# A streaming encoder layer on one core: norm statistics and small level products issued in portions, mixer weights split in the first FFN, scores three blocks ahead

## The chip, the cores and the metric

The kernel runs on one core of a Trainium2 chip. The metric is the device time of one execution in microseconds; several executions are timed, and their median counts. One more execution is profiled: every instruction of the engines TensorE (PE, with its weight loads as PEld), VectorE (DVE), ScalarE (ACT), GpSimd (POOL) and the DMA queue of SyncE (SP) is recorded.

## What is computed

One inference step of an encoder layer on 1056 tokens (1024 of a prompt and 32 of a running stream), width 1024, all in fp32:

```python
x = x + 0.5 * swiglu(rmsnorm(x, g_ffn1), w1g, w1u, w1d)
mix, k, v, s = token_mixer(rmsnorm(x, g_mix), w_in, ...)
x = x + mix
x = x + 0.5 * swiglu(rmsnorm(x, g_ffn2), w2g, w2u, w2d)
return rmsnorm(x, g_final), k, v, s
...
def token_mixer(h, ...):
    q_sb, k_sb, v_sb, q_g, k_g, v_g, r_g, lr_g = jnp.split(h @ w_in, points, axis=-1)
    o_sb = rmsnorm(stick_breaking(rmsnorm(q_sb), rmsnorm(k_sb), v_sb))   # 8 heads x 64
    o_g = rmsnorm(gla_scan(q_g, k_g, v_g, log_a)) * silu(r_g)            # 4 heads, dk 64, dv 128
    return concat(o_sb, o_g) @ w_out
```

Stick-breaking attention takes, for each query, a sigmoid of each score times the product of (1 - sigmoid) over all later keys. The gated linear attention (GLA) is a scan over tokens with a decay for each key channel.

## The kernel before

**Number format.** Activations lie transposed: eight tiles `S.x[d]` of 128 channels x 1056 tokens. Matmuls take fp32r operands, and each fp32 operand is split into a high and a low half by `split_to`: ACT rounds to the high half, then DVE (or POOL, with `pool=True`) subtracts to get the low one. A product is three matmuls (`mm3`, L60 to L62): high x high, high x low, low x high.

**Stages.** First FFN (gate and up by Strassen steps in `gate_up`, then down), the mixer, the second FFN. In the mixer a slab of `w_in` (128 output channels, one of 24) is used by one projection (`proj`, tile `pj`): three chunks of 352 tokens, each eight `mm3`. `load_split` brings a slab as 512 KB into `S.raw`, and splits it into `whl`, one of two buffers of the pool `wp`; in the mixer the low half is POOL's (L53).

**What sets the order.** `run(items, filler)` issues a list of items (small dependent pieces: scores, transposes, level products) and strews fillers (one `mm3` of a projection, or one output group) among them in proportion to the weights given. Behind it the framework's scheduler may still reorder instructions that are ready. Each engine then runs its own queue strictly in that order, and SP issues all DMAs of the kernel in its own.

**GLA.** `gla_items` treats two heads at a time: the decay logits, then products of queries and keys at levels 6 to 0 (`level6` and `level5` as one piece each, on operands `M`), then states and outputs. It runs twice, with projections as filler.

**Attention.** Four pairs of heads, p = 0 to 3. `sb_project` makes q, k and v of the next pair as filler, while `sb_items` runs sixteen blocks of the current one. A `Block` has three parts: `scores` (matmuls `z`, two sigmoids on ACT, a scan L1206 and a product L1207 on DVE that give `w`), `turn` (transposes `tr` of `w`, split into `wt`) and `values` (matmuls `av`). Scores are issued two blocks ahead of the turns; `f` and `w` have two buffers each.

**Norms.** `Norm.stat` squares a head's output, sums over channels by nine narrow matmuls (`means`, tile `st`, L711, 18 in the profile), takes the power -1/2 on POOL (L701) and for pairs of heads spreads the result (L729). `Norm.apply` transposes it (L746) and multiplies (L749). Both are one piece each.

**The end of the mixer.** When the third pair is done, the gated GLA heads in `S.x[4..7]` are split into `S.h[4..7]`, all twelve pieces at once. During the fourth pair output groups (`out_group`, tile `po`, on slabs `wo` loaded and split by `slab_a`) are the filler, and `ready(k)` splits finished heads, one POOL operation each (L53, tile `h`).

**First FFN.** In `gate_up` each step has seven products (24 matmuls each, tiles `acc_a` to `acc_d`); the hidden parts that the down product needs are formed (`keep`), split and stored to `part_spill`, four of them in one burst after a step's last product, through four buffers `S.x[0..3]`.

Of the kernel before, what the change touches and what calls it, by code (L numbers as in the profile page):

```python
# [15 lines left out]
P = 128  # L16
# [21 lines left out]
def load_split(S, src, hi_pool, tag, pool=False):  # L38
# [5 lines left out]
    split_to(S, w[:, 0], w[:, 1], raw, pool)  # L44
    return w

# [227 lines left out]
class Step:  # L274
# [89 lines left out]
    def out(self, q, u, ps):  # L364
# [12 lines left out]
        else:  # L377
# [9 lines left out]
            if f in PLAIN:  # L387
                nc.sync.dma_start(S.hidden[PLAIN.index(f)][:, h * HALF : h * HALF + HALF], hid)
            elif q != 1:
                self.keep({0: "B11", 3: "B22", 2: "B21"}[q], hid)  # L390
            else:
                b11, b12, b21, b22 = (S.x[4 + n][:, :HALF] for n in range(4))
                for name, o, x, y in (("T1", b11, b12, b11), ("T3", b12, b22, b12), ("T2", b22, b22, b11), ("T4", b21, b21, b22)):
                    nc.vector.tensor_sub(o, x, y)  # L394
                    self.keep(name, o)

    def keep(self, name, src):
# [16 lines left out]
def gate_up(S, H, op, steps, among, between, tail, xd):  # L414
# [31 lines left out]
    for t in range(N):  # L446
        for p in ORDER:
            steps[t].product(p)
            steps[t].after(p)
            if p > 2:  # L450
# [217 lines left out]
def proj(S, src, cb):  # L668
# [4 lines left out]
    def one(c, k):  # L673
        def go():
            if "w" not in hold:
                hold["w"] = load_split(S, src, S.wp, "w", True)
# [28 lines left out]
def means(S, sq, ones, groups):  # L705

    nc = S.nc
    st = S.pst.tile([P, CW], F32, name="st", tag="st")
    for b in range(NB + 1):
        n = P if b < NB else DEC  # L710
        nc.tensor.matmul(st[:n, groups * b : groups * b + groups], sq[:, b * P : b * P + n], ones[:, :: P // groups], start=True, stop=True)  # L711
    return rsqrt(S, st, groups)


class Norm:
# [6 lines left out]
    def stat(self):  # L722
        S = self.S
        sq = square_buf(S)
        S.nc.scalar.activation(sq, self.t, AF.Square)
        self.r = means(S, sq, self.ones, self.groups)
        if self.groups > 1:
            r, f = self.r, P // self.groups
            spread = lambda t, r: S.nc.gpsimd.tensor_copy(t.rearrange("p b (g f) -> p b g f", f=f), r.unsqueeze(3).broadcast_to([*r.shape, f]))  # L729
            big = S.nbuf[1] if S.nbuf else S.big.tile([P, NR], F32, name="nR", tag="b")  # L730
            self.r = big[:, :SEQ].rearrange("p (b f) -> p b f", f=P)
            self.last = S.tmp.tile([DEC, 1, P], F32, name="nL", tag="nL", bufs=1)
            spread(self.r, r[:, :NB])
            spread(self.last, r[:DEC, NB:])
# [15 lines left out]

    def parts(self):
        return [(4, self.stat), (4, self.apply)]
# [55 lines left out]
def gla_qk(S, A, hp):  # L808
    nc = S.nc
    qg, kg = S.x[4 + 2 * hp], S.x[5 + 2 * hp]  # L810
    q = proj(S, A["win"][12 + hp], lambda c, ps: nc.scalar.activation(qg[:, cs(c)], ps, AF.Copy, scale=0.125))
    k = proj(S, A["win"][14 + hp], lambda c, ps: nc.vector.tensor_copy(kg[:, cs(c)], ps))
# [3 lines left out]
def gla_v(S, A, hp, vs):  # L816
# [11 lines left out]
    return [proj(S, A["win"][16 + 2 * hp + h], put(h)) for h in range(2)]  # L828


def gla_items(S, A, G, hp, vs):
# [54 lines left out]
    def level6():  # L886
        M, ps = T.M[6], pair("g6")
        for b in range(NB):
            o = b * P
            for h in range(2):  # L890
# [870 lines left out]
```

## Time and profile before

| | us |
|---|---|
| three runs: median (lowest to highest) | 2154.25 (2153.37 to 2156.0) |
| profiled execution, its own time | 2149.15 |
| its span, first to last instruction | 2147.4 |
| mean granted clock of TensorE | 0.988 |

The profile's page gives each engine's busy time, and groups of instructions by line; "idle before" is the engine's idle time just ahead of a group and what ended it. The windows view gives busy time in stretches of the span, and the clock that was granted there. The timeline lists instructions in order, with the idle time before each in brackets. Lines (L53) are those of the kernel before.

### The profile page before, as it was taken

What the parts mean: (1) busy time and instruction counts of PE and PEld (TensorE: products, weight loads), DVE (VectorE), ACT (ScalarE), POOL (GpSimd) and SP (SyncE); (2) the same over time, 40 slices, a digit from 0 to 9 for tenths busy, and PEclk for the clock granted to TensorE, in tenths of its full rate; (3) what the DMA queues carried; (4) which work ended last, traced back from release to release, by engine and by line L of the source; (5) the groups of instructions that cost most, each with busy time, mean ns of one, the idle gap of its engine ahead of it and who ended that gap; (6) DMA issues with size and microseconds to landing.
All of it is one profiled execution on the core that took longest, in us unless ns stands there. A gap on an engine that the chain in (4) does not pass through costs nothing.

```text
span 2147.4 us, 38446 instructions
## 1 busy us (share of the span) xinstructions
PE 2069.2 (96%) x15636; PEld 1998.0 (93%) x15636; DVE 1442.3 (67%) x2142; ACT 892.2 (42%) x1586; POOL 742.8 (35%) x609
## 2 busy tenths in 40 slices
PE   7999999999999999999999988899999999999997
PEld 6899999999999978888888987899999999999997
DVE  6856756646786766286776687687567667467865
ACT  6533433432233443335555555454334333322333
POOL 0134334345872321122223312101343343458720
PEclk9999999999999999999999999999999999999999
DMA  5134434449823200102203141231344334498322
GB/s 174 50 120 152 161 121 154 168 139 379 303 94 117 87 32 30 38 31 67 77 23 100 36 124 69 78 123 51 120 159 156 127 143 168 139 376 300 106 65 82
DMA packets 106705, 270.49 MB, mean 126 GB/s; under 512 B 10432, under 2 KB 31200, under 8 KB 106528
## 3 DMA queue, kind: packets, MB, share of 16 engines
q1 hardware_dynamic: 106528, 268.03, 35.6%
q8 instruction: 123, 2.02, 0.4%
q14 instruction: 54, 0.44, 0.1%
HBM read 174.46 MB, written 86.77 MB: 122 GB/s over the span
## 4 chain that ended last, share of the span: by engine, by line
PE 77%; DVE 13%; ACT 3%; issue 3%; DMA 2%; POOL 1%; DVEq 0%; SPq 0%; ACTq 0%; POOLq 0%
PE acc_a L335 11%; PE acc_c L335 11%; PE acc_d L335 11%; PE acc_b L335 5%; PE acc L243 4%; PE pj L60 3%; PE pj L61 3%; PE pj L62 3%; PE pd_c L516 3%; PE pd_a L516 2%; PE pd_d L516 2%; DVE f L1206 2%; PE pd L60 2%; PE pd L62 2%; PE pd L61 2%
## 5 line engine op out<-in xcount | busy, mean ns | idle before, releaser
L335 PE MATMUL acc_a<-h,whl 128*128 128x264 f32 x1920 | 250.1, 286 | 1.8 <-DVE whl L55 1.8
L335 PE MATMUL acc_d<-part,S 128*128 128x264 f32 x1920 | 246.6, 284 | 0.0
L335 PEld LDWEIGHTS acc_a<-h,whl 128*128 128x128 f32 x1920 | 241.6, 190 | 2.1 <-DVE whl L55 2.1
L335 PEld LDWEIGHTS acc_d<-part,S 128*128 128x128 f32 x1920 | 238.7, 188 | 0.0
L60 PE MATMUL pj<-h,whl 128*128 128x352 f32 x576 | 203.9, 354 | 0.0
L61 PE MATMUL pj<-h,whl 128*128 128x352 f32 x576 | 191.1, 332 | 0.0
L62 PE MATMUL pj<-h,whl 128*128 128x352 f32 x576 | 190.8, 331 | 0.0
L51 ACT ACTIVATE S<-s 128x512 fp32r<-128x512 f32 x160 | 98.7, 627 | 183.6 <-PE acc_d L335 77.0
L51 ACT ACTIVATE x<-x 128x528 fp32r<-128x528 f32 x112 | 72.4, 647 | 180.8 <-DVE x L394 84.8
L319 POOL TENSOR_TENSOR s<-wraw,s 128x512 f32<-128x512 f32 x38 | 49.1, 1292 | 278.9 <-DVE S L55 278.9
L385 POOL TENSOR_TENSOR x<-tc,x 128x528 f32<-128x528 f32 x60 | 103.6, 1727 | 120.0 <-DVE tc L384 107.4
L53 POOL TENSOR_TENSOR whl<-wraw,whl 128x1024 fp32r<-128x1024 f32 x28 | 69.4, 2480 | 169.9 <-ACT whl L51 169.8
L55 DVE TENSOR_TENSOR x<-x 128x528 fp32r<-128x528 f32 x112 | 85.3, 761 | 63.1 <-ACT x L51 60.8
L335 PE MATMUL acc_b<-h,S 128*128 128x264 f32 x960 | 125.5, 286 | 1.5 <-ACT h L51 1.1
L335 PE MATMUL acc_c<-part,S 128*128 128x264 f32 x960 | 124.3, 284 | 0.3 <-DVE hid L255 0.3
L55 DVE TENSOR_TENSOR S<-s,S 128x512 fp32r<-128x512 f32 x160 | 122.0, 763 | 3.7 <-ACT S L51 2.5
L335 PE MATMUL acc_c<-h,A 128*128 128x264 f32 x960 | 124.2, 285 | 0.0
L335 PEld LDWEIGHTS acc_b<-h,S 128*128 128x128 f32 x960 | 121.2, 189 | 1.9 <-ACT h L51 1.3
L534 POOL TENSOR_TENSOR x<-x,u 128x528 f32<-128x528 f32 x64 | 103.5, 1624 | 49.5 <-DVE x L505 49.0
L335 PEld LDWEIGHTS acc_c<-part,S 128*128 128x128 f32 x960 | 120.0, 188 | 0.6 <-DVE hid L255 0.6
L335 PEld LDWEIGHTS acc_c<-h,A 128*128 128x128 f32 x960 | 120.4, 188 | 0.0
L306 POOL TENSOR_TENSOR s<-wraw 128x512 f32<-128x512 f32 x38 | 48.9, 1288 | 195.6 <-DVE S L55 195.6
(344 smaller groups left out, 5122.4 us busy)
## 6 DMA issues: line engine op xcount, KB each, us to landing
part_spill<-x SPq DMA_DIRECT2D x112, 528.0 KB, 2.8
h<-part_spill SPq DMA_DIRECT2D x64, 528.0 KB, 8.9
part<-part_spill SPq DMA_DIRECT2D x48, 528.0 KB, 9.6
wraw<-win SPq DMA_DIRECT2D x24, 512.0 KB, 3.4
wraw<-w1g SPq DMA_DIRECT2D x22, 512.0 KB, 3.7
wraw<-w1u SPq DMA_DIRECT2D x22, 512.0 KB, 3.4
wraw<-w1d SPq DMA_DIRECT2D x22, 512.0 KB, 3.8
wraw<-w2g SPq DMA_DIRECT2D x22, 512.0 KB, 3.5
```

Of the source, the lines that this page charges most:

```text
L51: nc.scalar.activation(hi, src, AF.Copy)
L53: nc.gpsimd.tensor_sub(lo, src, hi.bitcast(F32))
L55: nc.vector.tensor_sub(lo, src, hi.bitcast(F32))
L60: nc.tensor.matmul(out, w[:, 0, wsl], a[:, 0, asl], start=first, stop=False)
L61: nc.tensor.matmul(out, w[:, 0, wsl], a[:, 1, asl], start=False, stop=False)
L62: nc.tensor.matmul(out, w[:, 1, wsl], a[:, 0, asl], start=False, stop=last)
L243: nc.tensor.matmul(out, self.w[i](k, a), quarter(S, k, b, j), start=k == 0 and n == 0, stop=k == KT - 1 and n == 2)
L319: eng.tensor_sub(src, a12, self.s2)
L335: nc.tensor.matmul(t[:, s, :SW], w[:, a, ks], m(k, b, s), start=fresh and k == 0 and n == 0, stop=k == 3 and n == 2, skip_group_check=not ...
L385: nc.gpsimd.tensor_mul(two(hid), t, sg)
L516: nc.tensor.matmul(t[:, s, :SW], w[:, u, k * P : k * P + P], b[:, v, ss(s)], start=fresh and k == 0 and i == 0, stop=k == 1 and i == 2, sk ...
L534: nc.gpsimd.tensor_add(x[r][h], x[r][h], u)
```

## The change

It has six parts.

1. `Splits` takes 26 slabs in the first FFN's loop (22 of `w_in`, all but those of the first GLA q and k, and the first four of `w_out`), as 52 halves: load of 256 KB, split on ACT and DVE, store of 512 KB to `win_split` or `wo_split`, at slots counted in products. Its two buffers are `S.x[2]` and `S.x[3]`.
2. In the mixer `load_halves` loads a split slab, 1 MB, straight into `whl`. `S.raw` is only open in the FFNs, and its room goes to a third buffer of `f` and `w`.
3. `form` spreads the hidden parts over the following two steps, through two buffers.
4. `means` and `Norm.stat` return three items of three matmuls each, and `spread_in` puts them among the projections. `level6` and `level5` become items of four blocks, and a pad of weight 24 stands before them in the first GLA run.
5. Scores run three blocks ahead.
6. The gated heads are split by chunk in the filler (`gated`), the finished heads by chunk on DVE (`ready(k, c)`), and the third pair's norm is spread among the output groups.

```diff
+def load_halves(S, src, pool, tag):
+    w = pool.tile([P, 2, 1024], F32R, name="whl", tag=tag)
+    S.nc.sync.dma_start(w.bitcast(F32), src)
+    return w
...
+class Splits:
+        for n in range(2 * len(jobs)):
+            slot = 5 * n // 2
+            for k, fn in ((0, self.load), (3, self.split), (4, self.store)):
+                self.at.setdefault(slot + k, []).append((fn, n))
...
+    def load(self, n):
+        self.S.nc.sync.dma_start(self.buf(n)[:, 512:], self.jobs[n // 2][0][:, self.cols(n)])
+    def split(self, n):
+        t = self.halves(n).bitcast(F32R)
+        split_to(self.S, t[:, 0], t[:, 1], self.buf(n)[:, 512:])
+    def store(self, n):
+        self.S.nc.sync.dma_start(self.jobs[n // 2][1][:, :, self.cols(n)], self.halves(n))
...
-        t = S.x[S.n_kept % 4].bitcast(F32R).rearrange("p (a n) -> p a n", a=2)
+        t = S.x[S.n_kept % 2].bitcast(F32R).rearrange("p (a n) -> p a n", a=2)
...
+FORMS = [{1: [(1, "B21")], 3: [(1, "T1")], 5: [(1, "T3")]}, {0: [(2, "T2")], 2: [(2, "T4")], 4: [(0, "B22")], 6: [(0, "B11")]}]
...
+            for back, name in FORMS[t % 2].get(n, ()):
+                if t >= back:
+                    steps[t - back].form(name)
...
+            chore(7 * t + n)
...
+    def some(b0):
+        def go():
+            for b in range(b0, b0 + 3):
+                nc.tensor.matmul(out, hold["sq"][:, b * P : b * P + n], ones[:, :: P // groups], start=True, stop=True)
+            if b0 == 6:
+                put(rsqrt(S, hold["st"], groups))
+        return 2, go
+    return [some(b0) for b0 in (0, 3, 6)]
...
+def spread_in(items, at, step, more):
+    for n, x in enumerate(more):
+        items.insert(at + n * (step + 1), x)
...
-    items += [(6, level6), (6, level5)]
+    if not early:
+        items.append((24, lambda: None))
+    items += [(3, level6(b0)) for b0 in (0, 4)] + [(3, level5(b0)) for b0 in (0, 4, 8, 12)]
...
+    spread_in(pk[0], 2, 3, means(S, lambda: T.sq, S.ones64, 2, scales))
+    for n in norms[1:]:
+        spread_in(pk[1], 0, 3, n.stat())
+        pk[2][4:4] = [(4, n.apply)]
...
-        if n + 2 < len(blocks):
-            items.append((w, blocks[n + 2].scores))
+        if n + 3 < len(blocks):
+            items.append((w, blocks[n + 3].scores))
...
+            jobs = [(A["win"][i], A["win2"][i]) for i in range(24) if i not in (12, 14)]
+            jobs += [(A["wo"][i], A["wo2"][i]) for i in range(4)]
+            splits = Splits(S, jobs, (S.x[2], S.x[3]))
...
+                def gated(c):
+                    for k in (6, 7, 4, 5):
+                        split_to(S, hi, lo, o)
...
-                S.att, S.big, S.wt = pool("att", 2), pool("big", 2), pool("wt", 3)
-                fills = [gate(2), gate(0), gate(1) + gate(3)]
+                S.att, S.big, S.wt = pool("att", 2), pool("big", 3), pool("wt", 3)
+                g1, g3 = gate(1), gate(3)
+                fills = [flat(gate(2)), flat(gate(0)), flat([g1[c] + g3[c] + [(0, lambda c=c: gated(c))] for c in range(NCH)])]
...
-                        slabs[j] = load_split(S, A["wo"][j], S.wp, "w", True)
+                        slabs[j] = load_halves(S, A["wo2"][j], S.wp, "w")
...
-                            split_to(S, S.h[k][:, 0], S.h[k][:, 1], S.x[k], True)
+                        def ready(k, c):
+                            split_to(S, S.h[k][:, 0, cs(c)], S.h[k][:, 1, cs(c)], S.x[k][:, cs(c)])
...
+                        spread_in(fill, 1, 1, prev.stat() + [(4, turned)])
+                        for n in range(9):
+                            fill.insert(10 + n, (1, lambda n=n: ready(n // 3, n % 3)))
```

Where the scheduler puts this, three places show. POOL's queue in the second half of the attention, before (`whl` is a slab's low half, `f` a block's border, `nr` and `nv` the power of a norm):

```order
L1194 MEMSET f 128x1 x5
L53 TENSOR_TENSOR whl<-wraw,whl 128x1024
L1194 MEMSET f 128x1
L53 TENSOR_TENSOR whl<-wraw,whl 128x1024
L1194 MEMSET f 128x1
L701 TENSOR_TENSOR nr<-nv,mhalf 128x18
L729 COPY x<-nr 128x1024
L729 COPY nL<-nr 32x128
L697 MEMSET nv 128x18
L1194 MEMSET f 128x1 x4
L1249 MEMSET fs 32x2
L53 TENSOR_TENSOR whl<-wraw,whl 128x1024
```

And POOL after the change, at the same place:

```order
L1302 MEMSET f 128x1 x5
L759 TENSOR_TENSOR nr<-nv,mhalf 128x18
L812 COPY x<-nr 128x1024
L812 COPY nL<-nr 32x128
L755 MEMSET nv 128x9
L1302 MEMSET f 128x1 x4
L1357 MEMSET fs 32x2
L1302 MEMSET f 128x1 x2
L759 TENSOR_TENSOR nr<-nv,mhalf 128x18
L1201 TENSOR_SCALAR rn<-nr 128x18
L755 MEMSET nv 128x18
```

The slab splits are gone; what is left on POOL is borders, powers and copies. Next TensorE in the attention of the second pair, before (`st` is a statistic, `tr` and `av` the turns and values, `z` scores, `pj` a projection):

```order
L1218 MATMUL tr<-consts,w 128x128
L711 MATMUL st<-consts,x 128x2 x8
L711 MATMUL st<-consts,x 32x2
L1231 MATMUL av<-wt,vs 128x256 x14
L1231 MATMUL av<-wt,vs 128x128 x2
L1199 MATMUL z<-ks,qh 128x384
L1200 MATMUL z<-ks,ql 128x384
L1202 LDWEIGHTS identb
L1202 MATMUL z<-maskb,identb 128x128
```

TensorE after the change, around the second portion of the same kind of statistic:

```order
L103 MATMUL pj<-h_86,whl 128x352
L104 MATMUL pj<-h_86,whl 128x352
L105 MATMUL pj<-h_86,whl 128x352
L1307 MATMUL z<-ks,qh 128x512
L1308 MATMUL z<-ks,ql 128x512
L1310 LDWEIGHTS identb
L1310 MATMUL z<-maskb,identb 128x128
L1326 MATMUL tr<-consts,w 128x128 x2
L777 MATMUL st<-consts,x 128x2 x3
L103 MATMUL pj<-h_87,whl 128x352
L104 MATMUL pj<-h_87,whl 128x352
L105 MATMUL pj<-h_87,whl 128x352
```

The nine matmuls of the statistic stood in one run, and now come as three, three and three, some twenty instructions apart. In the GLA runs they still stand in one run of nine. Last DVE at the end of the third pair, before (`h_88` to `h_91` are `S.h[4..7]`, split in chunks of 352; `ks` is the next pair's key; L1517 and L1518 are a gate):

```order
L1137 TENSOR_TENSOR ks<-kf,ks 64x1056
L55 TENSOR_TENSOR wt<-tr,wt 128x4x128
L55 TENSOR_TENSOR h_90<-x,h_90 128x352
L55 TENSOR_TENSOR h_88<-h_88 128x352
L55 TENSOR_TENSOR h_89<-h_89 128x352
L55 TENSOR_TENSOR h_88<-h_88 128x352
L55 TENSOR_TENSOR h_89<-h_89 128x352
L1178 TENSOR_TENSOR x<-avt,av 64x256
L1517 TENSOR_TENSOR rs<-rs,pj 128x352
L55 TENSOR_TENSOR h_88<-h_88 128x352
L1518 TENSOR_TENSOR x<-x,rs 128x352
L55 TENSOR_TENSOR h_89<-h_89 128x352
```

DVE after the change, where the first chunk's gated heads are split:

```order
L1628 TENSOR_TENSOR rs<-rs,pj 128x352
L98 TENSOR_TENSOR h_90<-x,h_90 128x352
L1629 TENSOR_TENSOR x<-x,rs 128x352
L98 TENSOR_TENSOR h_88<-h_88 128x352
L98 TENSOR_TENSOR h_89<-h_89 128x352
L98 TENSOR_TENSOR h_91<-x,h_91 128x352
L1286 TENSOR_TENSOR x<-avt,av 64x256
L1244 TENSOR_TENSOR ks<-kf,ks 64x1056
L98 TENSOR_TENSOR h_85<-x,h_85 128x352
L1314 SCALAR_TENSOR_TENSOR f<-f 128x1024
L98 TENSOR_TENSOR wt<-tr,wt 128x4x128
L1315 TENSOR_TENSOR w<-w,f 128x1024
```

The splits of the gated heads stood next to each other behind the last `wt` splits; now each chunk's four come with its gate, among scans and `wt` splits, and pieces of `h_84` and `h_85` (the finished heads, POOL's before) lie between them.

More of the change, by code (lines that the diff above doesn't have):

```diff
@@ L411, in gate_up_steps, with gate_up @@
     return steps
-def gate_up(S, H, op, steps, among, between, tail, xd):
+def gate_up(S, H, op, steps, among, between, tail, xd, chore):
     N = len(steps)
@@ L702, in rsqrt, with means @@
     return r
-def means(S, sq, ones, groups):
+def means(S, sq, ones, groups, put):
     nc = S.nc
[L708 to L712, printed above, removed]
+    hold = {}
+    def some(b0):
+        def go():
+            if b0 == 0:
+                hold["sq"] = sq()
+                hold["st"] = S.pst.tile([P, CW], F32, name="st", tag="st")
+            for b in range(b0, b0 + 3):
+                n = P if b < NB else DEC
+                out = hold["st"][:n, groups * b : groups * b + groups]
+                nc.tensor.matmul(out, hold["sq"][:, b * P : b * P + n], ones[:, :: P // groups], start=True, stop=True)
[6 more added lines that the diff above has]
+        items.insert(at + n * (step + 1), x)
 class Norm:
@@ L826, in put @@
         return cb
[L828 removed]
+    return [proj(S, A["win2"][16 + 2 * hp + h], put(h)) for h in range(2)]
 def gla_items(S, A, G, hp, vs):
@@ L884, in pair @@
         return [S.pz.tile([P, 512], F32, name=name, tag="z") for _ in range(2)]
[L886 to L890, printed above, removed]
-                nc.tensor.matmul(ps[h][:64, b * 64 : b * 64 + 64], M[HS[h], o : o + 64], M[HS[h], o + 64 : o + P], start=True, stop=True)
-        for h in range(2):
-            nc.scalar.activation(T.AT[h][0:64, 0:NB, 64:P], ps[h][:64].rearrange("p (b t) -> p b t", b=NB), AF.Copy)
-        ahead(4)
@@ new lines, in level5, with go @@
+    def level5(b0):
+        def go():
+            if b0 == 0:
+                T.ps = pair("g5")
+            M, ps = T.M[5], T.ps
+            for b in range(b0, b0 + 4):
+                o = b * 64
+                for h in range(2):
+                    nc.tensor.matmul(ps[h][:32, b * 32 : b * 32 + 32], M[HS[h], o : o + 32], M[HS[h], o + 32 : o + 64], start=True, stop=True)
+            if b0 == 12:
+                for h in range(2):
+                    p4 = ps[h][:32].rearrange("p (b two t) -> p b two t", two=2, t=32)
+                    nc.scalar.activation(T.AT[h][0:32, 0:NB, 32:64], p4[:, :, 0], AF.Copy)
+                    nc.scalar.activation(T.AT[h][64:96, 0:NB, 96:P], p4[:, :, 1], AF.Copy)
+                ahead(3)
+        return go
@@ L1450, in between @@
                     emit(parts(H))
-            gate_up(S, H, op, steps, among, between, down.head, A["x"])
+            jobs = [(A["win"][i], A["win2"][i]) for i in range(24) if i not in (12, 14)]
+            jobs += [(A["wo"][i], A["wo2"][i]) for i in range(4)]
+            splits = Splits(S, jobs, (S.x[2], S.x[3]))
+            gate_up(S, H, op, steps, among, between, down.head, A["x"], splits.some)
             nc.vector.tensor_copy(S.identb, consts[:, 0])
@@ L1648, in between @@
                     emit(parts(H))
-            gate_up(S, H, op, steps, lambda j, n: [], between, down.head, xs)
+            gate_up(S, H, op, steps, lambda j, n: [], between, down.head, xs, lambda n: None)
             down.strassen(xs)
```

179 lines of the change are left out of this document (103 added, 76 removed).

## The prediction

> **What bounds the kernel now.** I read the page first, for the engine that sets the time.
>
> ```profile
> PE 2069.2 (96%) x15636; PEld 1998.0 (93%) x15636; DVE 1442.3 (67%) x2142; ACT 892.2 (42%) x1586; POOL 742.8 (35%) x609
> ```
>
> TensorE is busy for 96% of the span, and the change takes no matmul away (in the order of instructions the mixer has 1836 wide and 1710 small ones before and after). So it can win only TensorE's idle time and time at a lowered clock. The windows view, cut at the first scores of each pair of heads, tells where those are; its columns are stretch, length, busy us of PE, PEld, DVE, ACT and POOL, granted clock, DMA share and GB/s.
>
> ```profile
> 100.00:480.00 380.00, 380.00 (x3118) 380.00 (x3118) 236.03 (x302) 144.66 (x226) 157.08 (x107) 1.00 0.40 143
> 745.00:893.00 148.00, 139.89 (x957) 122.61 (x956) 79.49 (x126) 55.31 (x85) 28.55 (x16) 0.99 0.09 29
> 893.00:988.00 95.00, 91.74 (x672) 78.65 (x671) 65.93 (x124) 39.44 (x60) 19.40 (x15) 0.96 0.15 50
> 988.00:1076.00 88.00, 82.91 (x571) 76.02 (x571) 66.30 (x100) 53.71 (x113) 23.56 (x30) 1.00 0.23 65
> 1076.00:1167.00 91.00, 88.14 (x591) 81.02 (x591) 66.30 (x101) 53.37 (x112) 26.97 (x34) 0.96 0.15 47
> 1167.00:1284.00 117.00, 110.03 (x730) 103.68 (x729) 86.24 (x126) 66.02 (x136) 33.23 (x35) 0.97 0.31 88
> 1284.00:1378.00 94.00, 84.71 (x546) 76.17 (x544) 67.13 (x107) 47.32 (x99) 20.12 (x24) 0.95 0.15 53
> ```
>
> The first FFN's loop (first row) has no TensorE idle at all: nothing to win there, only to lose. The six mixer stages idle for 8.1, 3.3, 5.1, 2.9, 7.0 and 9.3 us, 35.6 in all, and their clock is below 1. That is the purse. Cut finer, the lowered clock turns out to be eight short windows at half rate between 745 and 1378:
>
> ```profile
> 1081.40:1084.80 3.40, 3.40 (x14) 3.40 (x13) 1.94 (x4) 1.19 (x3) 3.34 (x2) 0.50 0.27 104
> 1136.00:1139.40 3.40, 3.40 (x13) 2.81 (x12) 2.59 (x4) 2.54 (x5) 3.34 (x2) 0.50 0.00 0
> 1224.70:1228.10 3.40, 3.40 (x15) 3.34 (x14) 0.99 (x3) 0.60 (x1) 2.73 (x4) 0.51 0.00 0
> 1279.40:1286.20 6.80, 6.67 (x26) 6.60 (x27) 4.50 (x11) 3.48 (x8) 0.00 (x0) 0.50 0.67 239
> 1293.00:1296.40 3.40, 3.35 (x13) 2.90 (x14) 1.72 (x4) 0.00 (x0) 2.61 (x4) 0.50 0.14 20
> 1320.30:1323.70 3.40, 3.37 (x14) 2.91 (x13) 3.40 (x5) 1.64 (x3) 0.00 (x0) 0.50 0.01 5
> 791.30:794.70 3.40, 3.29 (x36) 2.72 (x35) 3.40 (x3) 1.72 (x3) 2.45 (x1) 0.51 0.00 0
> 900.50:907.30 6.80, 6.80 (x29) 6.25 (x30) 4.15 (x6) 1.75 (x2) 1.91 (x2) 0.50 0.15 59
> ```
>
> Half rate costs half the window: 1.7 us for 3.4, 3.4 for 6.8, 17 us in all. Idle and clock together are 52.6 us: no outcome of this change can win more than about that.
>
> **The change part by part.** *Splits off POOL (pre-split weights).* In the mixer POOL makes the low half of each slab, and DVE wants the same stretch of time. First at 993, in the timeline (start, length, engine, idle before and who ended it):
>
> ```profile
> 992.26 2.38 POOL L53 TENSOR_TENSOR whl<-wraw,whl 128x1024 fp32r<-128x1024 f32 x1
> 993.06 1.86 DVE L1206 TENSOR_TENSOR_SCAN f<-f 128x128 f32<-128x128 f32 x1 [1.57 <-ACT f L1203]
> 995.49 0.30 PE L1218 MATMUL tr<-consts,w 128*128 128x128 f32 x1 [1.46 <-DVE w L1207]
> ```
>
> ```profile
> 1288.47 0.40 DVE L1206 TENSOR_TENSOR_SCAN f<-f 128x128 f32<-128x128 f32 x1
> ```
>
> The same scan takes 0.40 us elsewhere and 1.86 beside a split: it ends with the POOL operation, and TensorE waits the 1.46 us that it grew by. Two more such places, the first in the linear attention, the second in the last pair:
>
> ```profile
> 792.17 2.86 DVE L876 TENSOR_TENSOR M<-M,x 128x512 f32<-128x512 f32 x1
> 795.17 1.51 PE L901 MATMUL g<-M 64*32 64x32 f32 x64 [0.58 <-DVE M L876]
> 798.88 1.30 PE L925 MATMUL gr<-M 64*128 64x128 f32 x11 [1.04 <-DVE M L876]
> ```
>
> ```profile
> 1315.79 2.79 DVE L1207 TENSOR_TENSOR w<-w,f 128x896 f32<-128x896 f32 x1
> 1319.37 0.44 PE L1218 MATMUL tr<-consts,w 128*128 128x128 f32 x2 [2.37 <-DVE wt L55]
> 1354.06 1.08 DVE L1207 TENSOR_TENSOR w<-w,f 128x896 f32<-128x896 f32 x1
> ```
>
> L1207 grew by 2.79 - 1.08 = 1.7 us. All slab splits but those of the first q and k leave the mixer, so these waits go: 1.46 + 0.58 + 1.04 + 1.7 = **4.8 us**. What is late next at 1319 is the scan itself, and the 0.7 left of that wait I leave standing.
>
> The price is paid in the first FFN: 52 half slabs, each a split on ACT and DVE and two DMAs.
>
> ```profile
> L55 DVE TENSOR_TENSOR S<-s,S 128x512 fp32r<-128x512 f32 x160 | 122.0, 763 | 3.7 <-ACT S L51 2.5
> part_spill<-x SPq DMA_DIRECT2D x112, 528.0 KB, 2.8
> ```
>
> A split of that shape takes DVE 0.763 us: 52 make 40 us, or 80 if each were held up to twice its length beside POOL, and DVE's 236 of 380 us become 276 (316). ACT, at 145, gets no more than that. Both keep gaps. The halves move 52 x 0.79 MB = 41 MB, 107 GB/s on top of 143, so a DMA share near 0.70 by the row's 0.40. A half comes every 2.5 products of 24 matmuls (380 / 3118 x 24 = 2.9 us by the first row of the windows), and an accumulator is next written two products after its last read is due; that 5.9 us is the cover. If it failed, every wait there would add to the end. I take 0 (the row's idle time is 0), with 10 us as the high end. The hidden parts, split in one burst before, are spread over two steps and use two buffers instead of four; a store lands in 2.8 us and a buffer comes round after four products, so that is 0 too.
>
> In the mixer a slab's load is now 1 MB and starts only when the slab two before it is done. Counted in the order, with 0.16 us for a wide matmul (the 0.122 of the first windows row x 352/264), this leaves 14 us or more, but 7.1 at the last gate slab and 6.5 at the first output slab. 528 KB land in 2.8 us, so twice that, 5.6, is my estimate: 0, and 3 us as the other end.
>
> *Gated heads and finished heads split in pieces.* At the end of the third pair the twelve gated splits and two POOL splits of whole heads fall together:
>
> ```profile
> 1270.85 0.52 DVE L55 TENSOR_TENSOR h<-x,h 128x352 fp32r<-128x352 f32 x1
> 1273.05 2.32 DVE L55 TENSOR_TENSOR h<-x,h 128x352 fp32r<-128x352 f32 x1
> 1275.40 3.35 DVE L1137 TENSOR_TENSOR ks<-kf,ks 64x1056 fp32r<-64x1056 f32 x1
> 1279.53 1.76 PE L1231 MATMUL av<-wt,vs 128*128 128x256 f32 x7 [4.62 <-DVE wt L55]
> 1288.62 3.27 POOL L701 TENSOR_TENSOR nr<-nv,mhalf 128x18 f32<-128x18 f32 x1 [10.98 <-DVE nv L699]
> 1293.05 1.97 PE L746 MATMUL tr<-consts,x 128*128 128x128 f32 x8 [2.16 <-POOL x L729]
> ```
>
> POOL's splits of two whole heads (`ready` in the code) stretch two DVE operations by 1.8 and 2.1 us, and the 4.62 us wait is these 3.9 plus 0.7. In the new order the pieces go to DVE (nine of 0.52 us: 4.7 us of DVE, about what the vanished stretches free) and lie among its other work: 3.9 of 4.62 goes. The 2.16 is a norm whose power on POOL takes 3.27 us with one output group in front of its transposes; now 21 wide matmuls, two blocks' scores and some values lie there, longer than the power and the copy behind it: it goes. **6.0 us**.
>
> *Scores three ahead.* The waits view has what this is for:
>
> ```profile
> PE tr L1218 <- DVE w L1207: 8.0, 12, 1.5
> ```
>
> 8.0 us in 12 waits; 1.46 of it is the case of 995, costed above. Of the other 6.5 I take half, **3.3**, because in the last pair DVE is nearly full:
>
> ```profile
> 1299.00:1362.00 63.00, 56.27 (x365) 49.52 (x365) 55.39 (x80) 38.79 (x84) 7.34 (x15) 0.97 0.10 37
> ```
>
> 55.4 of 63 us, with the nine head pieces partly to come: a block scored sooner there mostly queues sooner.
>
> *Statistics in portions.* No time is saved in the 18 narrow matmuls themselves. What they do is this:
>
> ```profile
> 1133.18 2.05 PE L711 MATMUL st<-consts,x 128*128 128x2 f32 x18
> ```
>
> At 1136.0 the clock drops; the windows at 1081.4 and 1224.7 follow such runs of 18 too. In the attention stages the order shows them now in threes with projections between. In the gated linear attention it doesn't: there the portions still stand together, so the window of 900.5 stays. The windows at 1279.4, 1293.0 and 1320.3 follow the long waits costed above. The six windows that can go are 5 x 1.7 + 3.4 = 11.9 us. Other such runs are followed by no window, so where one falls is partly luck, and I take three quarters: **8.9 us**.
>
> The Trainium skill (TensorE: Matmul & The Clock Gate, Part 1) has the gate drop after an idle window of about 3.4 us. That speaks against this edit: the run at 1133.18 has no idle time in it, and by that rule only the wait of 4.62 us could lower the clock, so 3.4 us of these 8.9 would be left and the time would come out at 2136.8. The trace, with 0.50 granted from 1136.0, decides for the other.
>
> *Small level products in portions, with a pad of weight 24.* The order shows only three more wide matmuls before the level of 64 (60, then 63), 0.5 us at 0.16 each; with as much for the other levels **1.0**.
>
> *What it costs on TensorE.* The mixer's wide matmuls are interrupted 289 times where it was 271. The first wide matmul after small ones is the slower one to follow:
>
> ```profile
> L60 PE MATMUL pj<-h,whl 128*128 128x352 f32 x576 | 203.9, 354 | 0.0
> L61 PE MATMUL pj<-h,whl 128*128 128x352 f32 x576 | 191.1, 332 | 0.0
> ```
>
> 12.8 us more for the first of each three, over at most 271 interruptions: some 0.05 us each, so **1.0 us** lost for 18.
>
> **Sum:** 4.8 + 6.0 + 3.3 + 8.9 + 1.0 - 1.0 = 23.0 us. The profiled execution took 2149.15 us (span 2147.4), 5.1 below the median of the three runs, so I carry the difference: 2154.25 - 23.0 = 2131.3, say 2131.
>
> **The rivals.** *The FFN pays (slower).* A half's split stands in ACT's queue and waits for its load, which SP issues only after the store two halves before it has landed. Spills of the same size take 8.9 us where the DMA engines are full:
>
> ```profile
> h<-part_spill SPq DMA_DIRECT2D x64, 528.0 KB, 8.9
> ```
>
> From a store's issue to the split two halves later are four products, 11.7 us. If a store came to 8.9 and the load behind it to half of that, they would take 13.4, and ACT would stand 1.7 us for each half with PSUM reads behind it; from there the rival decides. With a third of it reaching TensorE, 0.6 us for each of 52 halves, it takes 31 us and eats the 23: 2162. Against it: the share stays near 0.70. The Trainium skill (SBUF — State Buffer, the part on the shared port pair) has DVE and POOL lock each other out for a whole instruction, which the 1.86 us at 993 bears out; by it the splits moved into a loop where POOL is busy 157 of 380 us are held up again, and DVE goes towards the 316 worked out above, still below 380. *Waits only move (small gain).* In the last pair DVE, not TensorE, is the limit, portions that a scheduler puts together do nothing, and clock windows fall elsewhere: keep the 4.8 and half of the 6.0, lose 1.0: 6.8 us, 2147.5. *The change doesn't do what it says:* the new DMAs and queue order take back what is won, 2154.
>
> **How the numbers follow.** The main case has 0.64, the small gain 0.17, no change 0.10, the slower rival 0.09. About 0.2% (4.3 us) can be told from no change; the first two cases are faster by more: 0.81. The low end takes every named term in full and some small waits too, 40 us: 2114. The high end takes in the small gain and most of no change: 2152.
>
> **What would show it.** In the new profile the loop of the first FFN keeps PE at 380 of 380 with DVE near 276; POOL has no slab split between 800 and 1380, and no DVE scan is twice its usual length; the wait of 4.6 us before the last values of the third pair is under 1.5; half-rate windows after statistics in the attention stages are gone and the one near 900 remains. I am wrong if TensorE waits in the first FFN, if projections wait for `whl`, or if the transposes of the last pair wait as long as before.

## The result and the profile after

The changed kernel took 2159.82 us (median of 11 runs, 2155.39 to 2166.66), the kernel before 2152.12 us (11 runs, 2147.97 to 2156.0). The ratio is 1.0037, with a 95% interval of 1.0023 to 1.005: slower by 0.37%. The forecast was 2131 us, faster, with a range of 2114 to 2152. The rival in which the first FFN pays had been given 2162 us and a chance of 0.09.

The page of the kernel after: the lines that answer to those shown of before, and two groups of TensorE's products, which run in both FFNs (busy time, mean, and the idle time ahead of them):

```profile
span 2161.8 us, 38696 instructions
...
PE 2067.5 (96%) x15636; PEld 1997.3 (92%) x15636; DVE 1454.9 (67%) x2205; ACT 887.7 (41%) x1618; POOL 668.8 (31%) x578
...
L378 PE MATMUL acc_a<-h,whl 128*128 128x264 f32 x1920 | 251.4, 287 | 11.5 <-ACT s L391 9.5
...
L378 PE MATMUL acc_c<-h,A 128*128 128x264 f32 x960 | 126.7, 288 | 10.1 <-DVE u L397 9.8
```

The same two groups on the page before:

```profile
L335 PE MATMUL acc_a<-h,whl 128*128 128x264 f32 x1920 | 250.1, 286 | 1.8 <-DVE whl L55 1.8
L335 PE MATMUL acc_c<-h,A 128*128 128x264 f32 x960 | 124.2, 285 | 0.0
```

TensorE's share is the same 96%, and that hides two things of opposite sign. The table cuts the profiled executions at first and last matmuls: of the first FFN's loop (`acc_a` and the like), and of the mixer (first projection to last output group). Each column is a difference of two such times in the trace. "Half rate" is half the length of the windows with a granted clock of 0.5 inside the mixer.

| profiled execution | first FFN | mixer | the rest | half rate in the mixer |
|---|---|---|---|---|
| before (2149.15) | 417.8 | 698.6 | 1031.0 | 17.1 |
| after (2163.55) | 448.7 | 682.9 | 1030.2 | 15.4 |
| difference | +30.9 | -15.7 | -0.8 | -1.7 |

So the mixer gained much of what was forecast, and the first FFN, where "nothing to win" had been priced at nothing to lose, paid twice that. (The profiled run after is 3.7 us above its median and that of before 3.0 below: 14.4 us apart, where the medians are 7.7 apart. In which stage the others differ isn't known.)

The windows view of the first FFN after, its columns as in the prediction:

```profile
87.00:194.00 107.00, 100.58 (x799) 99.53 (x798) 78.10 (x101) 46.02 (x77) 40.66 (x28) 0.98 0.72 251
194.00:309.00 115.00, 106.60 (x844) 104.55 (x843) 75.46 (x100) 46.86 (x80) 42.75 (x28) 0.99 0.72 255
309.00:400.00 91.00, 82.51 (x665) 81.21 (x665) 66.37 (x86) 39.10 (x67) 36.35 (x23) 1.00 0.77 273
400.00:470.00 70.00, 70.00 (x576) 69.96 (x575) 46.64 (x61) 26.98 (x44) 27.46 (x18) 1.00 0.46 170
```

TensorE idles for 6.4, 8.4 and 8.5 us in the first three stretches and not at all in the fourth. (Of the 30.9 us in the loop 24.3 are idle time between matmuls, summed over the trace; the other 6.6 are in matmuls that take longer. About 3 us of these lie in two windows of 3.4 us at half rate, below; for the rest no view names a cause.) The DMA share falls at 400 from 0.77 to 0.46: the last half is split at 389.5, though the code spreads them over nearly the whole loop. DVE, at most 0.73 busy, isn't full.

```profile
143.00:146.40 3.40, 3.40 (x18) 3.40 (x17) 1.83 (x4) 2.97 (x5) 2.47 (x2) 0.50 0.59 180
231.80:235.20 3.40, 3.40 (x17) 3.34 (x16) 3.40 (x6) 1.56 (x3) 0.00 (x0) 0.50 0.86 332
```

The waits of the same stretch (90 to 500; total us, times, longest):

```profile
ACT x L94 <- DMA x<-win: 57.0, 24, 5.9
...
ACT x L94 <- DMA part_spill<-x: 18.8, 12, 2.5
...
PE acc_c L378 <- DVE u L397: 9.8, 8, 2.3
...
PE acc_a L378 <- ACT s L391: 9.5, 6, 2.0
```

ACT stands 57.0 us at splits whose load hasn't landed, and TensorE waits where a PSUM bank hasn't been read yet, by ACT (L391) or DVE (L397). One wait behind a load, from the timelines of PE, SP, ACT and DVE:

```profile
210.73 3.21 PE L378 MATMUL acc_c<-h,A 128*128 128x264 f32 x24 [1.51 <-DVE u L397]
...
201.99 2.67 SPq L84 DMA_DIRECT2D win_split<-x  x2
205.15 3.18 SPq L77 DMA_DIRECT2D x<-win  x2
...
208.71 0.63 ACT L94 ACTIVATE x<-x 128x512 fp32r<-128x512 f32 x1 [4.30 <-DMA x<-win]
...
209.37 0.69 DVE L98 TENSOR_TENSOR x<-x 128x512 fp32r<-128x512 f32 x1 [4.04 <-ACT x L94]
209.98 0.70 DVE L397 TENSOR_TENSOR u<-u,acc_c 128x528 f32<-128x528 f32 x1
```

SP issues a half's store at 201.99 and, once it has landed, the next load into the same buffer at 205.15. ACT has come to that load's split at 204.41 and stands 4.30 us; DVE's part of the split stands behind it, and the read of `acc_c` (L397) behind that. A second wait, some products later, when DVE's reads are late (that of `acc_d` at 224.63, 7.6 us after the product's end, where the kernel without halves, e1 below, takes 2.3), with POOL's rows:

```profile
230.68 4.71 PE L378 MATMUL acc_a<-h,whl 128*128 128x264 f32 x24 [1.94 <-ACT s L391]
...
224.40 0.62 ACT L94 ACTIVATE S<-s 128x512 fp32r<-128x512 f32 x1
229.48 0.64 ACT L94 ACTIVATE x<-x 128x528 fp32r<-128x528 f32 x1 [4.46 <-issue]
230.03 0.59 ACT L391 ACTIVATE s<-acc_a 128x528 f32<-128x528 f32 x1
...
225.85 1.83 DVE L98 TENSOR_TENSOR x<-x 128x512 fp32r<-128x512 f32 x1
227.61 2.53 DVE L442 TENSOR_TENSOR x<-x 128x528 f32<-128x528 f32 x2
...
225.41 1.73 POOL L428 TENSOR_TENSOR x<-tc,x 128x528 f32<-128x528 f32 x1 [2.11 <-DVE tc L427]
227.10 1.73 POOL L355 TENSOR_TENSOR s<-wraw,wraw 128x512 f32<-128x512 f32 x1
```

`acc_a` is needed back at 228.7. The read of it (230.03) stands in ACT's queue behind a form's split (229.48), which reads the difference made by DVE at L442 (227.61), which stands behind the second half of a slab's split on DVE (225.85, 1.83 us). (The row at 229.48 has "issue", no releaser; ACT's wait ends 0.04 us after the first L442, of 1.79 us.) A chain of queues, each in order. The chore is only part of it: the difference also needs POOL's product, which ends at 227.13, so the split in front cost it 0.5 us here; and DVE took 1.83 and 1.79 us beside POOL's operations, where the next L442, of the same shape, takes 0.71.

In the mixer, waits of the transposes for DVE's `w` fell from 8.0 us to 1.3, the 4.6 us wait of the third pair went, and POOL has no slab split (busy 80 of 683 us, 157 of 699 before). But a new wait leads (767 to 1430):

```profile
PE tr L831 <- POOL x L812: 12.7, 5, 5.8
PE tr L1326 <- DVE wt L98: 3.3, 4, 1.6
```

Before there was one such wait, of 2.16. The longest, in the last pair, by its rows on PE, POOL and DVE:

```profile
1326.63 1.12 PE L831 MATMUL tr<-consts,x 128*128 128x128 f32 x4 [5.83 <-POOL x L812]
...
1320.18 5.30 POOL L759 TENSOR_TENSOR nr<-nv,mhalf 128x18 f32<-128x18 f32 x1 [1.30 <-DVE nv L757]
1325.54 1.04 POOL L812 COPY x<-nr 128x1024 f32<-128x1024 f32 x1
...
1319.37 0.14 DVE L756 TENSOR_SCALAR nv<-st 128x16 f32<-128x16 f32 x1
```

The last portion of the statistic ended at 1314.0, DVE came to it 5.4 us later behind its scans, POOL's power took 5.30 us (3.22 to 3.27 in most of the others), then the copy. The 21 wide matmuls that the prediction counted did lie in between, with scores and values, and were done at 1320.8.

### The profile page after: what moved, and what is told of

The parts are those of the page before. It is cut to its first block, busy times and chain, and to the rows that moved or that the text cites. A ratio compares the mean times of both kernels' runs of the same rounds, so it can differ in the third digit from the quotient of the medians.

```text
span 2161.8 us, 38696 instructions
## 1 busy us (share of the span) xinstructions
PE 2067.5 (96%) x15636; PEld 1997.3 (92%) x15636; DVE 1454.9 (67%) x2205; ACT 887.7 (41%) x1618; POOL 668.8 (31%) x578
## 4 chain that ended last, share of the span: by engine, by line
PE 69%; DVE 11%; DMA 7%; issue 6%; POOL 4%; ACT 3%; SPq 0%; DVEq 0%; ACTq 0%; POOLq 0%
PE acc_a L378 8%; PE acc_d L378 8%; PE acc_c L378 7%; PE acc L286 4%; PE pj L103 4%; PE acc_b L378 4%; PE pj L105 3%; PE pj L104 3%; PE pd_c L574 3%; PE pd_d L574 3%; PE pd_a L574 3%; PE pd L103 2%; PE pd L105 2%; PE pd L104 2%; DMA win_split<-x 2%
## 5 line engine op out<-in xcount | busy, mean ns | idle before, releaser
L94 ACT ACTIVATE x<-x 128x528 fp32r<-128x528 f32 (+1 forms) x164 | 103.4, 638 | 295.8 <-POOL x L428 81.5
L98 DVE TENSOR_TENSOR x<-x 128x528 fp32r<-128x528 f32 (+1 forms) x164 | 132.1, 814 | 132.7 <-ACT x L94 132.0
L103 PEld LDWEIGHTS pj<-h,whl 128*128 128x128 f32 x576 | 110.5, 192 | 5.1 <-issue 1.7
```

The lines of the kernel that those rows point to most:

```text
L94: nc.scalar.activation(hi, src, AF.Copy)
L98: nc.vector.tensor_sub(lo, src, hi.bitcast(F32))
L103: nc.tensor.matmul(out, w[:, 0, wsl], a[:, 0, asl], start=first, stop=False)
```

## The experiments

Differences are against the changed kernel. Lines of the profile are those of each kernel. "FFN" and "mixer" are as in the table above.

**Which part of the first FFN's chore costs.** Four kernels: all splits but the first slab's left out (e1), loads and stores alone (e2), splits alone (e3), and splits one product later (e4).

```
e1  for k, fn in ((0, self.load), (3, self.split), (4, self.store)):   for n > 1: none of them
e2  for n > 1: load and store only      e3  for n > 1: split only
e1-e3: every projection that reads a pre-split slab reads A["win2"][0]
e4  ((0, self.load), (4, self.split), (5, self.store))
```

> Leaves out the splitting of all slabs but the first in the first FFN; every later projection of the mixer reads that one slab, in the same way and of the same size. From its first acc product to its last the first FFN took 417.7 us before and 448.7 after. Theory Q (the added loads, splits and stores are what costs, and the new places of the forms with two buffers in place of four cost nothing, as the second FFN already has them and takes the same 409.6 us): the FFN takes 416 to 419, PE waits there for ACT s and DVE u are gone, and the kernel is 12 to 18 us faster than before (2136). Rival F (the forms' new places and the two buffers cost it): the FFN stays at 440 or more.

> As the kernel without splits, but all 52 loads and 52 stores of halves are made, without the work on ACT and DVE between them (only the first slab is split). Theory Q (queueing of split, load and store behind each other in ACT, DVE and SP; neither part alone is dear): FFN at most 424. Rival D (the traffic: DMA share 0.72 where it was 0.38): FFN at 440 or more.

> As the kernel without splits, but all 52 halves are split on ACT and DVE, from what lies in the buffers, without loads and stores (those of the first slab are made). Theory Q: FFN at most 424, DVE busy some 36 us more in its loop. Rival C (the 52 instructions on ACT and DVE cost it, without the DMAs): FFN at 440 or more.

> The whole change, with each half split four products after its load and stored five after it (three and four in the change). Theory L (ACT stands at the split for its load, 57.0 us in 24 waits, and PSUM reads stand behind it): these waits fall below 25 us and the FFN to 435 or less, the kernel to 2148 or less. Rival (the waits are in the chain of store, load and split, which only moves): FFN 445 to 452, kernel within 0.2% of the change.

e1 took 2130.04 us, ratio 0.9897 (0.988 to 0.9914), FFN 416.9, mixer 679.5. So the forms' new places and two buffers cost nothing by themselves, and the rest of the change is worth 21.7 us, more than the 12 to 18 expected. e2: FFN 438.5, 2150.28. e3: FFN 436.2, 2145.41. (One run each.) Neither part is nearly free, so that half of theory Q fell, and neither reached its rival's 440. In e3 the whole loss lies in the first quarter of the loop's products, up to 205 us:

```profile
87.00:194.00 107.00, 97.47 (x754) 95.46 (x753) 103.37 (x124) 61.71 (x104) 40.41 (x25) 0.96 0.34 118
194.00:309.00 115.00, 111.27 (x900) 111.27 (x901) 74.49 (x97) 43.08 (x69) 47.20 (x31) 0.99 0.43 155
```

DVE is busy for 103.37 of 107 us: without loads to wait for, all 52 halves were split by 197 us, not where the code issues them. So e3 measures a crowd, not the splits' cost at their places. In e2 it was SP's queue that passed the delay on (first ACT's waits, then SP's own; L86 is a half's store):

```profile
ACT x L96 <- DMA part_spill<-x: 72.7, 22, 8.9
...
SPq L86 <- DMA x<-win: 46.9, 30, 4.2
```

A store that stands at SP for its load holds up the forms' stores behind it, and ACT stands for the forms' buffers. e4: 2161.25 us, 1.0043 (1.0028 to 1.0058), FFN 449.2: no change, its first theory was wrong.

**Slack, and three terms of the mixer.** e5 pre-splits 17 slabs instead of 26, more slowly; e8, e9 and e10 change the mixer of e1.

```
e5   slot = 15 * n // 4;  ((0, load), (4, split), (6, store));  slabs 0, 4, 8, 13, 15 to 19: load_split in the mixer
e8   fill.insert(9, (4, turned))      instead of right behind the last portion
e9   load_halves: + S.nc.gpsimd.tensor_add(lo, lo, lo)     lo = w[:, 1]
e10  blocks[n + 2].scores             instead of n + 3, no third block ahead of the loop
```

> The whole computation. 17 slabs (attention, gates, output) are split in the first FFN, one half per 3.75 products instead of 2.5, each split four products after its load and stored two later, so a buffer comes round in 7.5 products instead of 5; the nine slabs of the gated linear attention and of the first pair are split in the mixer on ACT and DVE through one raw buffer. Theory S (SP, whose queue is in order, stands at a store or load of the splits, 118 us in the change, and the forms' stores and the next loads stand behind it until ACT and DVE stand too): with the slack these waits go, the FFN takes at most 424 (448.7 in the change, 416.9 without splits) and the kernel 2130 to 2142. Rival W (each half has its price whatever the pace, 31.9 us for 52): FFN near 438, kernel near 2151.

> The kernel without splits in the first FFN, and the norm of the third pair is applied after output group 6 instead of group 4 of the last pair. Theory: the wait of its transposes for POOL's power and copy (5.83 us in the change, 2.16 before the change) comes from applying it too soon behind the last portion of its statistics; it falls under 1.5 us and the kernel is 3 to 6 us faster than the one without splits (2130.0). Rival: DVE, full there, is late anyway, and what is won comes back as waits of the blocks' transposes: within 1.5 us of it.

> The kernel without splits in the first FFN, and POOL makes one pass over each slab's low half after it is loaded (adds it to itself, so the low half is twice what it was), as POOL's split did before. This puts the first term of the prediction back by itself: 4.8 us by its sum, so 2134.8 against 2130.0. Rival: the stretched DVE operations (23 us of them before) cost more, 2140 or above; or nothing, within 1.5 us.

> The kernel without splits in the first FFN, with scores two blocks ahead as before. By the prediction's third term it is 3.3 us slower than 2130.0; rival: DVE decides in the last pair, and it is within 1 us.

e5: 2152.88 us, 0.9998 (0.9989 to 1.0006), FFN 437.2. That is rival W's number, but not its reason: quarter by quarter of the loop's products the FFN was 9.3 and 11.0 us slower than e1, then not at all for the second half. The halves had run as fast as in the change, and then there were none left. Theory S was wrong in that the slots in the code don't set the pace. The program's order on ACT shows it: between two first reads of `acc_a` (seven products) stand three to five halves, four on the mean, in the change as in e5, where the code gives 2.8 and 1.9. e8: 2124.51 us, 5.5 less than e1, and the wait of the last pair (5.3 us in e1) was gone. e9: 2144.17 us, 14.1 more than e1; 26 passes of 2038 ns:

```profile
L43 POOL TENSOR_TENSOR whl<-whl 128x1024 fp32r<-128x1024 f32 x26 | 53.0, 2038 | 208.5 <-DMA whl<-win_split 191.4 <-DVE w L1320 8.2 <-PE tr L1331 7.9
```

TensorE's waits in the mixer are 38.7 us there against 30.6 in e1, and half rate is 17.1 against 13.7. e10: 2125.24 us, 4.8 *faster* than e1; cut at the first `z` of each pair, it lost 3.8 us against e1 in the second pair and won 1.3, 1.2 and 6.4 in the first, third and last.

**The written order, the portions, the pieces.** e11 lets DVE, ACT and SP keep the order of the code in the first FFN; e12 adds e5, e8 and e10 to it; e13 and e14 change the mixer of e1.

```
e11  with tc.manual_schedule(engines={DVE, Activation, SP}):
         gate_up(S, H, op, steps, ..., splits.some)
e13  means: all nine blocks in the first portion, nothing in the other two
e14  ready: if c == 0: split_to(S, S.h[k][:, 0], S.h[k][:, 1], S.x[k], True)
```

> The whole change; in the first FFN DVE, ACT and SP keep the order in which the code issues their instructions. The program's order on ACT shows why two slacker paces changed nothing: the scheduler put four halves between two first reads of acc_a (one per step of seven products), 52 halves in the first 13 of 20 steps, whatever slot the code gave (e5_four_slots too: 34 in the first nine). In the written order they stand 2 to 3 to a step over all 20. Theory H (the halves are crowded by the scheduler): the FFN comes from 448.7 to 425 or less, the kernel to 2138 or less. Rival W (each half costs 0.6 us wherever it stands): FFN 445 or more.

> The whole computation: the 17 slabs of e5_four_slots in the written order, under 2 halves a step over the whole loop, the late norm of e8_late_turn and scores two ahead as in e10_two_ahead. Theory H: FFN at most 420 and, with the mixer of e8 and e10 (5.5 and 4.8 us under the kernel without splits, in part the same wait) and 2.4 us for the nine slabs that DVE splits in the gated linear attention, the kernel 2122 to 2130. Rival W: FFN 435 or more, kernel over 2140.

> The kernel without splits in the first FFN; each norm's statistic is made whole, 18 (or 9) narrow matmuls at the place of its first portion. By the prediction's fourth term (the portions save half-rate windows, 8.9 us) it is 5 to 9 us slower than 2130.0, with windows back behind the runs of 18. Rival P (the last portion stands closer to the transposes, which then wait for POOL's power, 12.7 us of such waits in the change, so portions cost more than they save): 3 to 8 us faster than 2130.0.

> The kernel without splits in the first FFN; in the last pair each of three finished heads is split whole, its low half on POOL, at the place of its first piece. By the second term of the prediction the pieces are worth up to 6.0 us, so 2133 to 2136 against 2130.0. Rival: DVE's nine pieces (0.5 us each) cost there what POOL's interference did, within 1.5 us.

e11 took 2164.09 us and e12 2155.99 (1.0018, 1.001 to 1.0026): worse than hoped, for one row at the loop's start:

```profile
113.36 0.81 PE L378 MATMUL acc_a<-h,whl 128*128 128x264 f32 x2 [22.91 <-ACT whl L94]
```

Behind it there is one wait in the loop, of 0.45 us; from the first product on the FFN took 412.5 us. The ordered stretch had taken in the opening, where the loop's first slab now stood behind all of the opening's conversions. e13: 2130.14 us, the same as e1, by two opposite terms. Of eleven runs of 18 in the attention five are followed by a half-rate window, and in three of these TensorE was busy for the whole 3.4 us ahead of it; one of them:

```profile
1030.00:1033.30 3.30, 3.30 (x28) 3.11 (x27) 1.40 (x3) 1.40 (x3) 0.00 (x0) 1.00 0.00 0
1033.30:1036.70 3.40, 3.40 (x17) 3.37 (x16) 0.57 (x3) 0.28 (x1) 3.12 (x2) 0.50 0.00 0
```

Half rate costs 18.8 us there, 13.7 in e1: the portions do save 5.1 us of clock. But the waits for POOL's copy, 12.2 us in e1, are zero in e13, and all waits in the mixer are 23.9 us instead of 30.6. e14: 2129.59 us, the same as e1: the pieces on DVE are worth nothing measurable.

**The loop alone.** e15, e16 and e17 meant to order the loop without its opening.

```
e15  gate_up(..., tc.manual_schedule(...))    with order:       around "for t in range(N)"
e16  e15, with e8 and e10       e17  e15, with e8;  pv[2][6:6], pk[2][7:7], pq[1][7:7]: the norms' apply later
```

> The whole change, with the loop of the first FFN alone (not its opening) in the written order on DVE, ACT and SP, so that the 52 halves stand 2 to 3 to a step in all 20 steps. Theory H (crowding by the scheduler): no wait over 0.5 us in the loop behind its start, the FFN 414 to 420, the kernel 2126 to 2134, all of the 21.7 us that the kernel without splits won. Rival: leaving the scheduler's order for ACT, DVE and SP costs other waits, or the start again: 2140 or more.

> As e15, with the late norm in the last pair and scores two ahead. If the two mixer savings (5.5 and 4.8 us alone) are partly the same wait, as in e12 (mixer 673.0 us with nine slabs split on DVE, against 679.5, 674.7 and 674.3), the mixer takes 670 to 673 and the kernel is 6 to 9 us faster than e15. Rival: in the pair before, scores two ahead cost the 5.7 us seen in e10 and e12 (a wait for POOL's power of 4.5 us), and it is within 4 us of e15.

> As e15, with scores three ahead, the late norm in the last pair, and the norms of the pairs before applied three or four projection steps (9 to 12 wide matmuls, 1.4 to 1.9 us) later. Theory P (the transposes come too soon behind the last portion, waits of 1.1 to 2.6 us each for POOL's power at four places in the change): these fall by 4 us or more in all, and the kernel is 8 to 11 us faster than e15. Rival: what comes later is then late for what is behind it (scores of the next pair), and it is 4 to 6 us faster, by the last pair alone.

All three kept the 22.9 us wait: 2167.32, 2161.84 and 2161.85 us. (e16 and e17 are each 5.5 us under e15, where 6 to 9 and 8 to 11 had been expected.) The program's order showed why: the ordered stretch begins where the object is made, which was still ahead of the opening. So e15 told nothing on its question. The mixer could be read: 681.8, 677.0 and 678.1 us. For e18 to e20 the object is made at the loop.

```
e18  gate_up(..., lambda: tc.manual_schedule(...))   with order():    e19  e18, with e8 and e10    e20  e19, with e17's norms
```

> The whole change, with the loop of the first FFN, and now only the loop, in the written order on DVE, ACT and SP; the opening is the scheduler's again. Theory H (crowding by the scheduler): no wait of 0.5 us in the loop, no 22.9 us at its start; FFN 415 to 421, kernel 2128 to 2136 (the kernel without splits took 2130.0). Rival W (the splits cost it wherever they stand): FFN 440 or more, kernel 2150 or more.

> As e18, with the late norm in the last pair and scores two ahead. The mixer of e16 took 4.8 us less than that of e15, so the kernel is 4 to 6 us faster than e18: 2123 to 2131. Rival: 2 us or less.

> As e19, with the norms of the pairs before applied later, as in e17. In e16 their transposes still wait 2.4, 4.5 and 2.9 us for POOL's power; in e17 such waits fell to 0.5 us but waits for DVE wt of 0.8 to 2.0 us stood at the same places. If half of the 9.8 us goes, the kernel is 3 to 6 us faster than e19; rival (the DVE waits take their place): within 2 us of it.

e18, the change with nothing but that order, took **2131.93 us**, 0.9898 (0.9881 to 0.9914). Its first FFN, by windows, and its waits on ACT and SP:

```profile
184.00:287.00 103.00, 103.00 (x847) 103.00 (x846) 83.25 (x99) 46.67 (x78) 40.99 (x28) 1.00 0.72 252
...
sum 406.00, PE 405.31 PEld 405.10 DVE 313.41 ACT 175.99 POOL 168.57; mean PE 81.06 PEld 81.02 DVE 62.68 ACT 35.20 POOL 33.72
...
ACT x L94 <- DMA x<-win: 28.3, 18, 4.2
...
SPq L77 <- DMA win_split<-x: 145.1, 37, 7.6
```

All 52 halves are there, the DMA share is the same 0.72 in the stretch shown, DVE is busier than in the change (313.41 us), SP stands 145.1 us for the halves' stores, ACT still 28.3 us for their loads, and TensorE loses 0.69 us. FFN 417.7, mixer 680.0. e19: 2128.27 us, 0.9882 (0.9867 to 0.9897), 3.7 less, under the 4 to 6 forecast. e20: **2116.92 us**, 0.9829 (0.9815 to 0.9844), mixer 664.0, half rate 8.5: 11.4 us under e19, where 3 to 6 had been expected, so the two edits that had looked alike (scores, norms) add up to more than either. e20 computes the whole reference and beats both kernels.

## Why the prediction was wrong

**The failing step** is the pace of the splits: "A half comes every 2.5 products of 24 matmuls", on which stands "I take 0" for the first FFN, and with it the ground on which the rival was set aside: "From a store's issue to the split two halves later are four products, 11.7 us." Four products is what the code's slots say. On ACT the scheduler put four halves to seven products, 1.75 each, so by that pace some 2.5 products are left, 7.3 us at the same 2.92 us each (an estimate). In the wait shown above it was less: ACT came to the split 2.4 us after the store's issue, and the store and the load took 6.7 us, quite without the 8.9 us of a full DMA that the prediction set as its condition. (On the page after a store takes 4.0 us and a load 3.6.) So the point from which the rival decides was already passed in the program's order, and that order could be read beforehand; it is quoted ahead of the prediction for the mixer, and the FFN was taken from the code. The rival's price (31 us, 2162) met the measurement (30.9 us, 2159.82), its condition didn't, so the price was luck in part: it came from a third of 1.7 us for each of 52 halves, where ACT stood 24 times for 2.4 us on the mean. The traffic, forecast at a share of 0.70, was 0.72.

What e18 adds is that the work and the traffic alone are not the cause: both are there, only the order differs, and it gives all of it back, FFN 448.7 to 417.7. The written order does two things at once. It thins the halves out to 2 or 3 a step. And it moves the forms: in the scheduler's order a form's split stands right before 8 of the 20 first reads of `acc_a` on ACT, in e18 before none. The forms' place isn't enough by itself. In e1, without halves, the same split stands before the same 8 reads, and TensorE doesn't wait:

```profile
213.37 0.65 ACT L96 ACTIVATE x<-x 128x528 fp32r<-128x528 f32 x1 [4.53 <-issue]
213.93 0.60 ACT L393 ACTIVATE s<-acc_a 128x528 f32<-128x528 f32 x1
...
218.24 3.10 PE L380 MATMUL acc_a<-h,whl 128*128 128x264 f32 x24
```

Nor is a half in front of a read enough: in e18 one stands right before 8 of the 20. In the change the loss lies where the two meet. Step by step against e1, with seven products to a step and the first step counted as 0, it loses 3.9 to 5.2 us in each of the steps 2, 4, 6, 8, 10 and 12, whose read has the form in front, and 1.9 us at most in the others; in steps 14 and 16, with the form and no halves left, it loses nothing. So the halves at the scheduler's pace are needed for the loss. Whether they would cost as much with the forms in their written places remains open; e5 doesn't tell, since its pace stayed the scheduler's.

**The mixer**, forecast at 23.0 us less with everything counted, came out at 21.7 (e1) and 21.1 (e18) by medians of the whole kernel (19.1 and 18.6 in the mixers of the profiled executions), near the forecast as a sum and not in its terms. That the sum is near is luck:

| term | forecast | part undone on top of e1 | measured |
|---|---|---|---|
| slab splits off POOL | 4.8 | e9 | 14.1 |
| pieces instead of whole heads | 6.0 | e14, the last pair's three heads only | -0.4 |
| scores three ahead | 3.3 | e10 | -4.8 |
| statistics in portions | 8.9 | e13 | 0.1 |

The first was sized from four waits that could be named in one trace; POOL's passes also lengthen DVE's operations (busy 477.8 us in the mixer of e9, 458.6 in that of e1), with small waits all over (8.1 us more in all), and 3.4 us more of half rate. Here the sum by named waits was a low bound. In the second the 4.6 us wait did go, but it stays away in e14 too, so the pieces aren't what removed it; where the gate's splits now stand wasn't tried. In the third the waits for `w` went, by more than forecast (8.0 to 1.3), and the new waits for the norm behind them were left out of the sum. With the norm late and applied later (e20) two ahead was kept, and three ahead wasn't tried beside it. In the fourth the mechanism was right (whole runs of 18 cost 5.1 us of clock in e13), though half rate in the change itself fell by 1.7 us alone, and the edit's other end was missed: between the last portion and the transposes there are now four to seven pieces of a projection where there were eight, and POOL's power takes 3.2 us of that. The prediction had said of the 2.16 us wait that enough work lay there now, and compared it with the power and the copy alone; DVE's 5.4 us ahead of them were left out, and it became 5.83. The two small terms for level products and interruptions weren't tried alone; interruptions rose by 18 in the trace, as forecast. The four measured terms come to 9.0 us, so 12 to 13 us of the gain are assigned to no part. Some 8 us of it are in TensorE's busy time, mostly of small matmuls that follow each other (118 ns each before and 115 after, outside the half-rate windows), and not in waits.

**The signs that were named:** TensorE in the FFN loop at its full time: wrong. DVE near 276 of 380 us there, 40 more than before: over the whole loop 255.0 us before became 291.0 in the change, 36 more. The Trainium skill (SBUF — State Buffer, Who interferes with whom) would have it go towards 80 more as DVE and POOL lock each other out; the change doesn't show that, and e18, with 313.41 and so 58 more, goes about half the way. No slab split on POOL, no wait of 4.6 us, a window near 900 (924.7 and 938.3 in the longer execution): right. Half-rate windows after statistics gone: partly; one follows a run of 18 still whole at 1007, and two of double length in the last pair follow the new waits. The Trainium skill (TensorE: Matmul & The Clock Gate, Part 1), by whose idle window most of this term would have come to nothing, isn't borne out by e13, where three windows follow 3.4 us in which TensorE never idled.

## What to carry to other kernels

Slots that the code gives to a chore are a wish when a scheduler places the instructions: read the pace from the program's order on each queue, and ask of what stands in front of every PSUM read when its input will be there, before pricing a chore at nothing. If it is crowded, order that loop alone by hand. And when a statistic is cut into portions or moved back, move what uses it too: count from its last portion through each engine's queue to the first user.

## What the runs showed that was not expected

- Waiting as such was cheap: in e18 SP stood 145.1 us for stores and ACT 28.3 us for loads in a loop where TensorE lost 0.69 us. In the change ACT's 57.0 us went with 23.3 us of idle TensorE in three stretches.
- Twenty-six POOL passes of 2.04 us each, for which TensorE waited by name once, 0.7 us, cost 14.1 us.
- POOL's power on 128x18 took 3.22 to 3.27 us in most places, and 5.30 with a 2.00 us scan on DVE beside it.
